# Places modulo 256 bytes for split weights and sums in a two-layer hybrid block, and other orders for the second MLP's w2

## The chip, the cores and the metric

The kernel runs on one core of a Trainium2 chip. The time is the device time of one execution in microseconds, the median of several runs. A profile of one execution gives start and length of each engine's instructions. TensorE (PE) multiplies; VectorE (DVE) and ScalarE (ACT) prepare operands and take results out of PSUM; GpSimd (POOL) does little here; SyncE (SP) issues the loads of the weights.

## What is computed

Two layers on x of 256 tokens by 2048 features, float32 throughout:

```python
def reference(x, ...):
    h = x
    for layer in range(2):
        if layer == 0:
            h = h + stick_breaking_attention(rms_norm(h, sb_norm_g[0]), sb_w_qkv[0], sb_w_out[0])
        else:
            h = h + native_sparse_attention(rms_norm(h, nsa_norm_g[0]), nsa_w_in[0], ..., nsa_w_out[0])
        h = h + sqrelu_mlp(rms_norm(h, mlp_norm_g[layer]), mlp_w1[layer], mlp_w2[layer])
    return h

def sqrelu_mlp(h, w1, w2):          # w1: 2048 x 8192, w2: 8192 x 2048
    return jnp.square(jax.nn.relu(h @ w1)) @ w2
```

The first attention has 16 heads of width 128; the second has 16 query heads in 4 groups with a compressed, a selected and a windowed branch and gates.

## The kernel before, in words

**Split operands.** TensorE multiplies float32 in a rounded form. The kernel writes each operand as a sum, hi + lo: hi is the rounded copy, lo the difference, rounded too. A product of two operands is then three products, hi by hi, lo by hi and hi by lo. For a weight this is done on the way: SP loads a piece of 512 KB into a `raw` tile (L132, five buffers), ScalarE copies it to `hi` (L125, four buffers), VectorE subtracts to `lo` (L127, four buffers), TensorE uses both. Activations lie split in `xs` (xhi and xlo side by side) and in `yhi` and `ylo`.

**Kinds of product.** Each product has a stationary operand of 128 by 128, loaded by a weight load (PEld), and a moving operand of 128 rows with up to 512 columns.
- Wide products with x (`proj_T2`, L193 and L199; `proj_T2h`, L213 and L219): the weight is stationary, xs moves. hi takes xhi and xlo at once, 512 columns; lo takes xhi alone, 256 columns.
- Ordinary chunks (`chunk_N`, L147): the weight moves, 512 columns, and x or y is stationary. A chunk is two rows of 128 of the weight by 512 columns, 12 products.
- Strassen chunks (`chunk_S`, L243 to L268): one of the four column blocks of w2 is multiplied by Strassen's scheme for two-by-two blocks, 7 products for 8, in 256 columns, so 21 with the split. VectorE makes four combinations of the weight's blocks in `ts` (L243, L247, L248), which are split like a weight into hi and lo (L125, L127). Three blocks go in without a combination: `shi` is their rounded copy (ScalarE, L246), `slo` their difference (VectorE, L249). `shi` and `slo` have one buffer each. The stationary operands are blocks of yhi and ylo and, for three of the seven pairs with a combination and one without, sums of y in the tile `ss`. So 12 of the 21 products have `ss`.

**The MLP.** Each layer's MLP runs over four quarters of the 8192 inner features. In a quarter, group1 makes the inner activations (four blocks of 512, each eight chunks of `proj_T2`), and squares, splits and sums them. group2 multiplies by w2: column blocks 0, 1 and 3 by ordinary chunks, block 2 by eight Strassen chunks spread among these. That is eight groups of eight Strassen chunks in the two layers.

**What sets the order.** TensorE's order is as written in the program. The tile framework's scheduler sets the orders of ScalarE, VectorE and SP from the dependencies between tiles: an instruction that writes a tile whose buffer is still read is placed, and waits, behind the last reader. Each engine then runs its instructions in that order. A tile is one unit for this: its last reader is the last reader of any part of it.

**Places.** The start of `xs`, `yhi` and `ylo` in each partition lies at 128 modulo 256 bytes; raw, hi, lo, `ts`, `shi`, `slo` and `ss` lie at 192.

Of the kernel before, what the change touches and what calls it, by code (L numbers as in the profile page):

```python
# [8 lines left out]
F32 = mybir.dt.float32  # L9
# [30 lines left out]
def hybrid_kernel(  # L40
# [8 lines left out]
    small = ctx.enter_context(tc.tile_pool(name="small", bufs=2))  # L49
    wraw = ctx.enter_context(tc.tile_pool(name="wraw", bufs=5))  # L50
# [15 lines left out]
    g0 = cpool.tile([KD, P], F32, name="g0")  # L66
    nc.scalar.dma_start(g0, sb_norm_g[0].rearrange("(k p) -> k p", p=P))
    grows = cpool.tile([P, P], F32, name="grows")
# [19 lines left out]
    def other_gains():  # L88
        nc.vector.memset(grows, 0.0)
        nc.sync.dma_start(grows[G_M0:G_NSA, :], mlp_norm_g.rearrange("l (k p) -> (l k) p", p=P))  # L90
        nc.sync.dma_start(grows[G_NSA:G_Q, :], grow(nsa_norm_g[0]))
        nc.sync.dma_start(grows[G_Q:G_K, :], nsa_q_norm_g)
        nc.sync.dma_start(grows[G_K:G_K + 3, :], nsa_k_norm_g[0])
        pgt = att.tile([P, NB], F32, tag="att", name="pgt2")
        nc.tensor.transpose(pgt[:, :P], grows, ident)
        nc.vector.tensor_copy(gT[:, KD:], pgt[:, KD:P])
        nc.vector.tensor_scalar(gq, gT[:, G_Q:G_K], SCALE, None, op0=OP.mult)
# [25 lines left out]
    def split(raw):  # L123
        hi = whi.tile(raw.shape, F32R, tag="hi", name="hi")
        nc.scalar.activation(hi, raw, AF.Copy)  # L125
        lo = wlo.tile(raw.shape, F32R, tag="lo", name="lo")
        nc.vector.tensor_tensor(lo, raw, hi.bitcast(F32), op=OP.subtract)  # L127
        return hi, lo

    def load(src, k0, nk, n0, nn):  # L130
        raw = wraw.tile([P, nk, nn], F32, tag="raw", name="raw")
        nc.sync.dma_start(  # L132
            raw, src[k0 * P:(k0 + nk) * P, n0:n0 + nn].rearrange("(k p) n -> p k n", p=P)
        )
        return raw

    def load_split(*where):
        return split(load(*where))
# [4 lines left out]
    def chunk_N(ps, src, k0, n0, first, last, ahi, alo, koff=0, by_token=False):  # L143

        hi, lo = src if isinstance(src, tuple) else load_split(src, k0, KC, n0, NB)
        tiles = [(kk, k0 - koff + kk, t) for kk in range(KC) for t in range(NT)]
        mm = lambda a, b, k, t, s, e: nc.tensor.matmul(ps[t], a[:, k, t * P:(t + 1) * P], b, start=s, stop=e)  # L147
        if by_token:

            half = [slice(0, NB // 2), slice(NB // 2, NB)]  # L150
            for t, c in [(0, slice(0, NB)), (1, half[0]), (1, half[1])]:
                for a, w in ((ahi, hi), (alo, hi), (ahi, lo)):
                    for kk in range(KC):
                        k = k0 - koff + kk
                        nc.tensor.matmul(
                            ps[t][:, c], a[:, k, t * P:(t + 1) * P], w[:, kk, c], start=False, stop=True,
                            skip_group_check=True,
                        )
            return
# [26 lines left out]
    def proj_T2(ps, src, n0):  # L186


        for k0 in range(0, KD, KC):
            hi, lo = load_split(src, k0, KC, n0, NB)  # L190
# [14 lines left out]
    def proj_T2h(src, n0):  # L205
# [3 lines left out]
        for k0 in range(0, KD, KH):  # L209
            hi, lo = load_split(src, k0, KH, n0, W)  # L210
# [23 lines left out]
    def chunk_S(ps, src, k0, n0, first, last, ahi, alo, shi, slo, koff=0):  # L234
# [9 lines left out]
        hi = wsum.tile([P, 3 * W], F32R, tag="shi", name="shi", bufs=1)  # L244
        lo = wsum.tile([P, 3 * W], F32R, tag="slo", name="slo", bufs=1)
# [40 lines left out]
    def add_S(nb, bs, ps, pool):  # L286

        W = NB // 2
        u = pool.tile([P, 2, W], F32, tag="u", name="u", bufs=1)
        v = pool.tile([P, 2, W], F32, tag="v", name="v", bufs=1)  # L290
# [127 lines left out]
    def mlp(l, layer, junk, done, last=None):  # L418
# [37 lines left out]
        def group2(fg, plain, strassen, end):  # L456
# [8 lines left out]
            for nb, i in order:  # L465
# [12 lines left out]
                if i == 0:  # L478
                    ps = [bank(*plain) for _ in range(NT)]
                out = last is not None and end and nb == 3  # L480
                chunk_N(ps, w2, k0, nb * NB, i == 0, i == NK - (2 if out else 1), yhi, ylo, koff=fg * KD,
                        by_token=out and i == NK - 1)
# [207 lines left out]
    pes = cpool.tile([2 * CL, P], F32, name="pes")  # L690
# [403 lines left out]
```

## Time and profile before

| | |
|---|---|
| time, median of 3 runs | 2201.65 us (2200.3 to 2204.76) |
| time of the profiled execution | 2201.79 us |
| its span | 2200.1 us |
| TensorE busy in the span | 2187.0 us (99%), 11922 products |
| VectorE, ScalarE busy | 1537.9 us (70%), 1204.4 us (55%) |
| first attention, 0 to 397 us: TensorE busy | 392.8 us |
| first MLP, 397 to 1100 us | 703.0 of 703.0 us |
| second attention, 1100 to 1490 us | 388.6 of 390.0 us |
| second MLP, 1490 to 2200 us | 702.6 of 710.0 us |

The profile's instructions are followed by their line in the kernel. The name of a tile stands without its buffer number: `att<-hi,ss` is a product into a PSUM bank of the pool att with moving operand hi and stationary operand ss. A product's recorded length holds its way through the array; products overlap, so their pace is read from one start to the next.

### The profile page before, as it was taken

How to read it: one execution, taken by the hardware profiler on the slowest of the kernel's cores; microseconds unless marked ns; L12 is line 12 of the kernel's file. 1: busy time of each engine (PE TensorE's matmuls, PEld its weight loads, DVE VectorE, ACT ScalarE, POOL GpSimd, SP SyncE). 2: the span in 40 equal slices, each digit the busy share in tenths (PEclk: the TensorE clock that was granted, in tenths of full speed). 3: DMA queues.
4: the chain of work that ended last, by engine and by line, in shares of the span. 5: the costliest groups of instructions: out<-in, count | busy, mean ns of one | idle time of the engine just before them, and what ended most of it. 6: DMA issues, size and time to landing. Idle time of an engine off the chain costs nothing.

```text
span 2200.1 us, 31289 instructions
## 1 busy us (share of the span) xinstructions
PE 2187.0 (99%) x11922; PEld 1875.4 (85%) x11922; DVE 1537.9 (70%) x2096; ACT 1204.4 (55%) x1697; POOL 42.6 (2%) x75
## 2 busy tenths in 40 slices
PE   9999999999999999999999999999999999999998
PEld 9888888888888888888887888888888888888887
DVE  5656655677667677668777777756776776777775
ACT  5565665555455455455555666655554554554553
POOL 0000000000000000000000011000000000000000
PEclk9999999999999999999999999999999999999999
DMA  7655555665665665665667554456556656656654
GB/s 233 207 165 172 165 171 182 182 192 184 205 190 175 215 190 178 215 191 174 213 184 219 153 144 139 134 169 183 181 183 214 188 184 207 189 174 220 189 174 155
DMA packets 260767, 405.98 MB, mean 185 GB/s; under 512 B 13188, under 2 KB 91912, under 8 KB 260616
## 3 DMA queue, kind: packets, MB, share of 16 engines
q1 hardware_dynamic: 259800, 403.52, 60.2%
q8 instruction: 93, 1.52, 0.3%
q10 hardware_dynamic: 816, 0.46, 0.1%
q14 instruction: 58, 0.48, 0.1%
HBM read 401.83 MB, written 2.10 MB: 184 GB/s over the span
## 4 chain that ended last, share of the span: by engine, by line
PE 98%; DVE 1%; DMA 0%; POOL 0%; ACT 0%; issue 0%; DVEq 0%; ACTq 0%; POOLq 0%
PE acc L147 31%; PE att L147 13%; PE acc L193 11%; PE att L193 11%; PE acc L213 5%; PE acc L199 5%; PE att L199 5%; PE att L268 4%; PE acc L268 3%; PE acc L219 3%; PE acc L176 2%; PE att L926 1%; PE att L331 1%; PE att L918 0%; DMA raw<-in_mlp_w_dram 0%; PE att L919 0%
## 5 line engine op out<-in xcount | busy, mean ns | idle before, releaser
L127 DVE TENSOR_TENSOR lo<-raw,hi 128x1024 fp32r<-128x1024 f32 x687 | 836.6, 1222 | 380.3 <-ACT hi L125 358.1
L125 ACT ACTIVATE hi<-raw 128x1024 fp32r<-128x1024 f32 x687 | 724.8, 1057 | 656.3 <-PE acc L147 208.5
L193 PE MATMUL acc<-xs,hi 128*128 128x512 f32 x1024 | 259.8, 396 | 0.0
L193 PE MATMUL att<-xs,hi 128*128 128x512 f32 x1024 | 259.1, 395 | 0.0
L147 PE MATMUL acc<-hi,yhi 128*128 128x512 f32 x640 | 251.7, 394 | 0.0
L147 PE MATMUL acc<-hi,ylo 128*128 128x512 f32 x640 | 250.6, 392 | 0.0
L193 PEld LDWEIGHTS acc<-xs,hi 128*128 128x128 f32 x1024 | 183.0, 188 | 34.7 <-DVE h L387 0.3
L193 PEld LDWEIGHTS att<-xs,hi 128*128 128x128 f32 x1024 | 183.2, 188 | 34.5
L147 PE MATMUL acc<-hi,xs 128*128 128x512 f32 x704 | 178.6, 394 | 0.0
L147 PE MATMUL acc<-lo,yhi 128*128 128x512 f32 x640 | 174.1, 393 | 0.0
L147 PEld LDWEIGHTS acc<-hi,xs 128*128 128x128 f32 x704 | 130.5, 188 | 27.6
L147 PE MATMUL att<-hi,ylo 128*128 128x512 f32 x380 | 149.7, 394 | 0.0
L147 PE MATMUL att<-hi,yhi 128*128 128x512 f32 x380 | 149.4, 393 | 0.0
L199 PEld LDWEIGHTS acc<-xs,lo 128*128 128x128 f32 x1024 | 135.9, 188 | 11.6
L199 PEld LDWEIGHTS att<-xs,lo 128*128 128x128 f32 x1024 | 135.9, 188 | 11.6
L147 PEld LDWEIGHTS acc<-lo,yhi 128*128 128x128 f32 x640 | 119.6, 188 | 25.8 <-issue 0.4
L147 PEld LDWEIGHTS acc<-hi,ylo 128*128 128x128 f32 x640 | 120.3, 188 | 24.5 <-DVE ylo L318 0.2
L147 PEld LDWEIGHTS acc<-hi,yhi 128*128 128x128 f32 x640 | 120.2, 188 | 24.3 <-ACT yhi L317 0.2
L199 PE MATMUL acc<-xs,lo 128*128 128x256 f32 x1024 | 137.6, 277 | 0.0
L199 PE MATMUL att<-xs,lo 128*128 128x256 f32 x1024 | 137.5, 277 | 0.0
L243 DVE TENSOR_TENSOR ts<-raw 128x512 f32<-128x512 f32 x64 | 44.3, 692 | 128.9 <-DMA raw<-in_mlp_w_dram 128.9
L125 ACT ACTIVATE hi<-ts 128x1024 fp32r<-128x1024 f32 x64 | 67.9, 1061 | 114.4 <-DVE ts L248 86.3
(305 smaller groups left out, 3064.9 us busy)
## 6 DMA issues: line engine op xcount, KB each, us to landing
raw<-in_mlp_w_dram SPq DMA_DIRECT2D x512, 512.0 KB, 4.2
raw<-in_sb_w_qkv_dram SPq DMA_DIRECT2D x95, 512.0 KB, 4.2
raw<-in_nsa_w_in_dram SPq DMA_DIRECT2D x50, 512.0 KB, 3.6
raw<-in_sb_w_out_dram SPq DMA_DIRECT2D x32, 512.0 KB, 3.9
raw<-in_nsa_w_in_dram SPq DMA_DIRECT2D x64, 256.0 KB, 3.4
raw<-in_nsa_w_out_dram SPq DMA_DIRECT2D x32, 512.0 KB, 3.9
w1t<-in_nsa_cmp_w_dram SPq DMA_DIRECT2D x8, 512.0 KB, 4.8
h<-in_x_dram SPq DMA_DIRECT2D x8, 256.0 KB, 4.5
```

Of the source, the lines that this page charges most:

```text
L125: nc.scalar.activation(hi, raw, AF.Copy)
L127: nc.vector.tensor_tensor(lo, raw, hi.bitcast(F32), op=OP.subtract)
L147: mm = lambda a, b, k, t, s, e: nc.tensor.matmul(ps[t], a[:, k, t * P:(t + 1) * P], b, start=s, stop=e)
L176: nc.tensor.matmul(o, w[:, kk, m * P:(m + 1) * P], x[:, k0 + kk, :], start=s, stop=e, skip_group_check=True)
L193: nc.tensor.matmul(ps[m], hi[:, kk, m * P:(m + 1) * P], xs[:, k0 + kk, :, :].rearrange("p a t -> p (a t)"), start=k0 + kk == 0, stop=k0 + ...
L199: nc.tensor.matmul(ps[m][:, :T], lo[:, kk, m * P:(m + 1) * P], xhi[:, k0 + kk, :], start=False, stop=k0 + kk == KD - 1, skip_group_check=True,
L213: nc.tensor.matmul(ps[m], hi[:, kk, m * P:(m + 1) * P], xs[:, k0 + kk, :, :].rearrange("p a t -> p (a t)"), start=k0 + kk == 0, stop=k0 + ...
L219: nc.tensor.matmul(ps[m][:, :T], lo[:, kk, m * P:(m + 1) * P], xhi[:, k0 + kk, :], start=False, stop=k0 + kk == KD - 1, skip_group_check=True,
L243: nc.vector.tensor_tensor(ts[:, :2, :], flat[:, W:3 * W].rearrange("p (a n) -> p a n", a=2), b12, op=OP.subtract)
L268: nc.tensor.matmul(ps[i], a, w, start=s, stop=e, skip_group_check=True)
L331: nc.tensor.transpose(ps[:, j * T + t * P:j * T + (t + 1) * P], h[:, t, (kp + j) * P:(kp + j + 1) * P], ident)
L926: nc.tensor.transpose(ptp[:w, j * P:(j + 1) * P], src(j), ident)
```

## The change

The tiles `hi` and `lo` get 64 elements of padding, and `split` takes an offset in elements for each: with 16 (FAR) the data starts at 192 modulo 256 bytes, as before, with 36 (NEAR) at 16. The wide products L193 and L213 use NEAR for hi and FAR for lo. The tile sizes move other tiles: `ss` now starts at 128, raw and `ts` at 128, and some small tiles of the second attention shift by 64; xs, yhi and ylo stay at 128. `shi` and `slo` become the halves of one tile `both` with one buffer, each half starting at 192. The two tiles u and v of `add_S` become one that shares its place with `pre`; the small tiles of gains and position rows share a place.

In the second layer's MLP, w2's ordinary chunks take their hi and lo at other places. In the first quarter column blocks 0, 1 and 3 have 128, 240 and 160; in the other three quarters 192, 128 and 240. In these three quarters the order of a chunk's twelve products changes too. Before, for each weight row and token half, hi·yhi and hi·ylo alternate, then the four lo·yhi follow. In the second quarter (way 1) all four hi·yhi, all four hi·ylo, then the four lo·yhi; in the third (way 2) the same sorted by token half; in the fourth (way 3) the three products of each pair follow each other. The last column block of the last quarter keeps its order.

```diff
@@ -47,6 +47,7 @@
     nc = tc.nc
     cpool = ctx.enter_context(tc.tile_pool(name="cpool", bufs=1))
     small = ctx.enter_context(tc.tile_pool(name="small", bufs=2))
+    small.tile([P, 48], F32, name="gap", bufs=1)
     wraw = ctx.enter_context(tc.tile_pool(name="wraw", bufs=5))
     whi = ctx.enter_context(tc.tile_pool(name="whi", bufs=4))
     wlo = ctx.enter_context(tc.tile_pool(name="wlo", bufs=4))
@@ -120,10 +121,17 @@
                 pass
 
-    def split(raw):
-        hi = whi.tile(raw.shape, F32R, tag="hi", name="hi")
+
+
+    PAD = 64
+    NEAR, FAR = 36, 16
+
+    def split(raw, o=(FAR, FAR)):
+        n = KC * NB
+        view = lambda t, a: t[:, a:a + n].rearrange("p (k n) -> p k n", k=raw.shape[1])
+        hi = view(whi.tile([P, n + PAD], F32R, tag="hi", name="hi"), o[0])
         nc.scalar.activation(hi, raw, AF.Copy)
-        lo = wlo.tile(raw.shape, F32R, tag="lo", name="lo")
+        lo = view(wlo.tile([P, n + PAD], F32R, tag="lo", name="lo"), o[1])
         nc.vector.tensor_tensor(lo, raw, hi.bitcast(F32), op=OP.subtract)
         return hi, lo
 
@@ -134,15 +142,15 @@
         )
         return raw
 
-    def load_split(*where):
-        return split(load(*where))
+    def load_split(*where, o=(FAR, FAR)):
+        return split(load(*where), o)
 
     def bank(pool, tag):
         return pool.tile([P, NB], F32, tag=tag, name=tag)
 
-    def chunk_N(ps, src, k0, n0, first, last, ahi, alo, koff=0, by_token=False):
-
-        hi, lo = src if isinstance(src, tuple) else load_split(src, k0, KC, n0, NB)
+    def chunk_N(ps, src, k0, n0, first, last, ahi, alo, koff=0, by_token=False, o=(FAR, FAR), way=0):
+
+        hi, lo = src if isinstance(src, tuple) else load_split(src, k0, KC, n0, NB, o=o)
         tiles = [(kk, k0 - koff + kk, t) for kk in range(KC) for t in range(NT)]
         mm = lambda a, b, k, t, s, e: nc.tensor.matmul(ps[t], a[:, k, t * P:(t + 1) * P], b, start=s, stop=e)
         if by_token:
@@ -157,6 +165,20 @@
                             skip_group_check=True,
                         )
             return
+        if way:
+            one = lambda a, w: [(a, w, kk, k, t) for kk, k, t in tiles]
+            order = one(ahi, hi) + one(alo, hi) + one(ahi, lo)
+            if way == 2:
+                order.sort(key=lambda x: x[4])
+            if way == 3:
+                order = [x for j in range(len(tiles)) for x in order[j::len(tiles)]]
+            seen = set()
+            for j, (a, w, kk, k, t) in enumerate(order):
+                mm(a, w[:, kk, :], k, t, first and t not in seen, last and all(x[4] != t for x in order[j + 1:]))
+                seen.add(t)
+            pump()
+            pump()
+            return
         for part in [tiles]:
             for kk, k, t in part:
                 mm(ahi, hi[:, kk, :], k, t, first and kk == 0, False)
@@ -187,7 +209,7 @@
 
         for k0 in range(0, KD, KC):
-            hi, lo = load_split(src, k0, KC, n0, NB)
+            hi, lo = load_split(src, k0, KC, n0, NB, o=(NEAR, FAR))
             tiles = [(kk, m) for kk in range(KC) for m in range(NB // P)]
             for kk, m in tiles:
                 nc.tensor.matmul(
@@ -207,7 +229,7 @@
         ps = [bank(acc, "acc") for _ in range(2)]
         KH, W = 2 * KC, NB // 2
         for k0 in range(0, KD, KH):
-            hi, lo = load_split(src, k0, KH, n0, W)
+            hi, lo = load_split(src, k0, KH, n0, W, o=(NEAR, FAR))
             tiles = [(kk, m) for kk in range(KH) for m in range(2)]
             for kk, m in tiles:
                 nc.tensor.matmul(
@@ -241,8 +263,8 @@
         ts = wsum.tile([P, 4, W], F32, tag="ts", name="ts")
         b12 = flat[:, 3 * W:].unsqueeze(1).to_broadcast([P, 2, W])
         nc.vector.tensor_tensor(ts[:, :2, :], flat[:, W:3 * W].rearrange("p (a n) -> p a n", a=2), b12, op=OP.subtract)
-        hi = wsum.tile([P, 3 * W], F32R, tag="shi", name="shi", bufs=1)
-        lo = wsum.tile([P, 3 * W], F32R, tag="slo", name="slo", bufs=1)
+        both = wsum.tile([P, 6 * W + PAD], F32R, tag="both", name="both", bufs=1)
+        hi, lo = [both[:, FAR + i * 3 * W:FAR + (i + 1) * 3 * W] for i in range(2)]
         nc.scalar.activation(hi, flat[:, :3 * W], AF.Copy)
         nc.vector.tensor_tensor(ts[:, 2, :], ts[:, 0, :], flat[:, 2 * W:3 * W], op=OP.add)
         nc.vector.tensor_tensor(ts[:, 3, :], flat[:, :W], ts[:, 2, :], op=OP.subtract)
@@ -286,8 +308,8 @@
     def add_S(nb, bs, ps, pool):
 
         W = NB // 2
-        u = pool.tile([P, 2, W], F32, tag="u", name="u", bufs=1)
-        v = pool.tile([P, 2, W], F32, tag="v", name="v", bufs=1)
+        uv = pool.tile([P, 4, W], F32, tag="pre", name="uv", bufs=1)
+        u, v = uv[:, :2, :], uv[:, 2:, :]
         hb = [h[:, t, nb * NB:(nb + 1) * NB] for t in range(NT)]
         nc.scalar.activation(u[:, 0, :], ps[0], AF.Copy)
         nc.vector.tensor_tensor(v[:, 0, :], ps[5], u[:, 0, :], op=OP.add)
@@ -478,8 +500,11 @@
                 if i == 0:
                     ps = [bank(*plain) for _ in range(NT)]
                 out = last is not None and end and nb == 3
+                a = 16
+                if l == 1:
+                    a = ((0, 28, 8), (16, 0, 28))[fg > 0][(0, 1, 1, 2)[nb]]
                 chunk_N(ps, w2, k0, nb * NB, i == 0, i == NK - (2 if out else 1), yhi, ylo, koff=fg * KD,
-                        by_token=out and i == NK - 1)
+                        by_token=out and i == NK - 1, o=(a, a), way=fg if l == 1 and not out else 0)
                 if i == NK - 1:
                     if out:
                         add_out(nb, ps, last)
```

The change moves instructions on VectorE and ScalarE around the Strassen chunks. This is VectorE in the first layer's third quarter, before. raw_7900 is the weight piece of the Strassen chunk that TensorE starts at 876.47 us, raw_7971 that of the next one, which it starts at 884.43 us; the `lo` from raw are of ordinary chunks between them:

```order
L243 TENSOR_TENSOR ts_7973<-raw_7971 128x512
L247 TENSOR_TENSOR ts_7973<-ts_7973,raw_7971 128x256
L249 TENSOR_TENSOR slo_7905<-raw_7900,shi_7904 128x768
L127 TENSOR_TENSOR lo_7939<-raw_7935,hi_7937 128x1024
L248 TENSOR_TENSOR ts_7973<-raw_7971,ts_7973 128x256
L127 TENSOR_TENSOR lo_7957<-raw_7953,hi_7955 128x1024
L127 TENSOR_TENSOR lo_7983<-ts_7973,hi_7981 128x1024
L243 TENSOR_TENSOR ts_8066<-raw_8064 128x512
L249 TENSOR_TENSOR slo_7976<-raw_7971,shi_7975 128x768
L127 TENSOR_TENSOR lo_8010<-raw_8006,hi_8008 128x1024
```

The same stretch of VectorE now; raw_7880 and raw_7950 are the two pieces, and L271 with the output `both` is the low half:

```order
L265 TENSOR_TENSOR ts_7952<-raw_7950 128x512
L269 TENSOR_TENSOR ts_7952<-ts_7952,raw_7950 128x256
L270 TENSOR_TENSOR ts_7952<-raw_7950,ts_7952 128x256
L135 TENSOR_TENSOR lo_7918<-raw_7914,hi_7916 128x1024
L271 TENSOR_TENSOR both_7884<-raw_7880,both_7884 128x768
L135 TENSOR_TENSOR lo_7936<-raw_7932,hi_7934 128x1024
L135 TENSOR_TENSOR lo_7961<-ts_7952,hi_7959 128x1024
L265 TENSOR_TENSOR ts_8044<-raw_8042 128x512
L135 TENSOR_TENSOR lo_7988<-raw_7984,hi_7986 128x1024
L271 TENSOR_TENSOR both_7954<-raw_7950,both_7954 128x768
```

The low half of each Strassen chunk stands one `lo` of an ordinary chunk further back, the first of the two also behind the last `ts` step. ScalarE in the same stretch, before:

```order
L125 ACTIVATE hi_7910<-ts_7902 128x1024
L246 ACTIVATE shi_7904<-raw_7900 128x768
L125 ACTIVATE hi_7937<-raw_7935 128x1024
L125 ACTIVATE hi_7955<-raw_7953 128x1024
L125 ACTIVATE hi_7981<-ts_7973 128x1024
L246 ACTIVATE shi_7975<-raw_7971 128x768
L125 ACTIVATE hi_8008<-raw_8006 128x1024
```

And now, where L268 is the high half in `both`:

```order
L133 ACTIVATE hi_7889<-ts_7882 128x1024
L133 ACTIVATE hi_7916<-raw_7914 128x1024
L268 ACTIVATE both_7884<-raw_7880 128x768
L133 ACTIVATE hi_7934<-raw_7932 128x1024
L133 ACTIVATE hi_7959<-ts_7952 128x1024
L133 ACTIVATE hi_7986<-raw_7984 128x1024
L268 ACTIVATE both_7954<-raw_7950 128x768
```

The high half too stands one copy of an ordinary chunk further back. The order of the loads on SP is the same.

More of the change, by code (lines that the diff above doesn't have):

```diff
@@ L65, in hybrid_kernel @@
     G_SB, G_M0, G_M1, G_NSA, G_Q, G_K = 0, KD, 2 * KD, 3 * KD, 64, 65
-    g0 = cpool.tile([KD, P], F32, name="g0")
+    g0 = small.tile([P, P], F32, tag="grow", name="g0", bufs=1)[:KD, :]
     nc.scalar.dma_start(g0, sb_norm_g[0].rearrange("(k p) -> k p", p=P))
-    grows = cpool.tile([P, P], F32, name="grows")
     grow = lambda g: g.rearrange("(k p) -> k p", p=P)
@@ L88, in other_gains @@
     def other_gains():
+        grows = small.tile([P, P], F32, tag="grow", name="grows", bufs=1)
         nc.vector.memset(grows, 0.0)
@@ L688, in hybrid_kernel @@
         out_proj(sb_w_out[0], "m0", G_M0)
-    pes = cpool.tile([2 * CL, P], F32, name="pes")
+    pes = small.tile([P, P], F32, tag="grow", name="pes", bufs=1)[:2 * CL, :]
     nc.scalar.dma_start(pes, nsa_cmp_pe[0].rearrange("a l d -> (a l) d"))
```

## The prediction

> **What bounds the kernel now.** I read the page first (busy shares, chain by engine), then the waits of TensorE, then the chain piece by piece for the pace of each kind of product, and last the timeline of one Strassen chunk on VectorE, TensorE and the DMA queue.
>
> ```profile
> PE 2187.0 (99%) x11922; PEld 1875.4 (85%) x11922; DVE 1537.9 (70%) x2096; ACT 1204.4 (55%) x1697; POOL 42.6 (2%) x75
> PE 98%; DVE 1%; DMA 0%; POOL 0%; ACT 0%; issue 0%; DVEq 0%; ACTq 0%; POOLq 0%
> PE acc L268 <- DVE slo L249: 3.4, 3, 2.6
> ```
>
> TensorE is busy for 99% of the span and is 98% of the chain that ended last. Its largest wait is 3.4 us in three places, all for the low half of a Strassen chunk. So two things can move the time: the pace of the products themselves, and new waits of TensorE for what VectorE and ScalarE prepare. The page's row of TensorE clocks is 9 in all slices, so no clock change lies in it.
>
> The change touches both. Pace first, from the chain of waits (start us, us, what):
>
> ```profile
> 584.29 1.86 PE att L193 x8
> 586.15 0.91 PE att L199 x8
> 131.47 10.08 PE acc L147 x44
> 871.14 5.49 PE acc L147 x24
> 876.63 2.46 PE att L268 x21
> ```
>
> A wide product with x (L193, 512 columns) takes 1.86/8 = 232.5 ns from start to start. A product of the ordinary w2 and projection chunks (L147, also 512 columns, also 128 by 128) takes 10.08/44 = 229.1 or 5.49/24 = 228.8 ns. Same size, same clock, 3.6 ns apart. What differs is where the operands lie (the places here are the start addresses that the two programs give their tiles): in L193 the moving operand (xs) lies at 128 modulo 256 bytes in each partition and the stationary one (hi) at 192; in L147 it is the other way round.
>
> **The change part by part.**
>
> *The wide products.* Their hi goes from 192 to 16, against xs at 128. No product of the kernel before has that pair of places, so the cost is bounded by the nearest rows.
>
> ```profile
> L193 PE MATMUL att<-xs,hi 128*128 128x512 f32 x1024 | 259.1, 395 | 0.0
> L213 PE MATMUL acc<-xs,hi 128*128 128x512 f32 x512 | 130.2, 396 | 0.0
> L193 PE MATMUL att<-xs,hi x1024: 388/396/398, 420.9 to 2081.7; 128*128 128x512 f32 x171
> ```
>
> There are 2 x 1024 of L193 (the other half writes acc) and 512 of L213: 2560 products. The third row gives shortest, median and longest. If each went as the shortest does, the gain is 8 ns each, 2560 x 8 = 20.5 us; if each went as the longest, a loss of 2 ns each, 5 us. I take the pace of L147, 3.6 ns less, because it is the same product size with its operands at another relation of places: 2560 x 3.6 = 9.2 us saved. A new hi place alters no instruction of ScalarE or VectorE, and these stages show no wait of TensorE for hi or lo, so the gain counts in full.
>
> *The sums of y.* ss goes from 192 to 128. In a Strassen chunk it is the stationary operand against moving operands at 192, that is, at the same place now, and 64 bytes apart after.
>
> ```profile
> L268 PEld LDWEIGHTS att<-hi,ss x192: 192/192/192, 501.7 to 2006.7; 128*128 128x128 f32 x192
> L268 PE MATMUL att<-hi,ss x192: 283/283/283, 501.9 to 2006.8; 128*128 128x256 f32 x192
> L268 PE MATMUL att<-shi,yhi x64: 276/276/276, 501.2 to 2005.8; 128*128 128x256 f32 x64
> L268 PE MATMUL att<-hi,yhi 128*128 128x256 f32 x32 | 8.8, 276 | 0.0
> ```
>
> Same line, the same moving tile hi, the same 256 columns: 283 ns against ss (at 192), 276 ns against yhi (at 128). Twelve of a chunk's 21 products have ss, over 64 chunks 768. At 7 ns each that is 5.4 us saved. This is the best supported term: after the change these products stand exactly as those with yhi do. Its bounds are 0 (should something other than the place make ss slow) and 5.4.
>
> Against both terms stands a rule of the Trainium skill, "SBUF — State Buffer", section "SBUF: two separate sides": TensorE's ports never wait on another user, and the table of the section after it gives the loading of weights a second, independent read port; by that rule the place of an operand is worth nothing and both terms are 0. The trace does not agree: 283 against 276 ns, with nothing but the stationary tile different. No page states a rule on places modulo 256 bytes.
>
> *The second layer's w2.* In its four groups hi and lo go to 128, 240 or 160 in the first group, and to 192, 128 or 240 in the other three, in which (but for the last block) the order of a chunk's twelve products changes too: by kind, by token, or per tile hi·hi, lo·hi, hi·lo. This is 1152 products of L147; 384 of them come to lie with both operands at 128. The nearest row with both operands at one place (192 both) and 512 columns is this:
>
> ```profile
> L642 PE MATMUL att<-sh,tri x8: 389/395/398, 99.0 to 330.5; 128*128 128x512 f32 x8
> L147 PE MATMUL acc<-hi,yhi 128*128 128x512 f32 x640 | 251.7, 394 | 0.0
> ```
>
> 395 against 394 ns: 1 ns on 384 products is 0.4 us. By the spread of the first row (389 to 398) the bounds on 1152 products are -5.8 to +4.6 us. I take +0.5. The third order asks for lo at the third product of a chunk and not at the ninth, six products or 1.4 us sooner. TensorE shows no wait for L127's lo today, so this is put at nothing; if that cover is gone it costs up to 1.4 us in each of the last group's 16 chunks of that order, and it is late there only where VectorE is late for the Strassen chunks too.
>
> *One tile for both halves.* This is not in the words of the change. shi and slo, two tiles of one buffer each, become the halves of `both`, one tile of one buffer. ScalarE's write of the next chunk's high half must now wait for the last product with the previous low half (the 17th of 21), not for the last one with the high half (the 6th). The scheduler answers by placing the high and low halves later on both engines: on VectorE a low part of an ordinary chunk (L127) now stands ahead of the Strassen low half. The chunk that TensorE starts at 884.43 us, on VectorE, on the DMA queue and on TensorE:
>
> ```profile
> 873.48 0.69 DVE L243 TENSOR_TENSOR ts<-raw 128x512 f32<-128x512 f32 x1 [2.61 <-DMA raw<-in_mlp_w_dram]
> 874.55 0.95 DVE L249 TENSOR_TENSOR slo<-raw,shi 128x768 fp32r<-128x768 f32 x1
> 875.42 1.22 DVE L127 TENSOR_TENSOR lo<-raw,hi 128x1024 fp32r<-128x1024 f32 x1
> 876.55 0.42 DVE L248 TENSOR_TENSOR ts<-raw,ts 128x256 f32<-128x256 f32 x1
> 883.96 0.69 DVE L243 TENSOR_TENSOR ts<-raw 128x512 f32<-128x512 f32 x1 [4.55 <-DMA raw<-in_mlp_w_dram]
> 884.57 0.95 DVE L249 TENSOR_TENSOR slo<-raw,shi 128x768 fp32r<-128x768 f32 x1
> 885.44 1.22 DVE L127 TENSOR_TENSOR lo<-raw,hi 128x1024 fp32r<-128x1024 f32 x1
> ```
>
> ```profile
> 875.53 0.37 SPq L132 DMA_DIRECT2D raw<-in_mlp_w_dram  x1
> 876.66 0.37 SPq L132 DMA_DIRECT2D raw<-in_mlp_w_dram  x1
> 878.13 0.37 SPq L132 DMA_DIRECT2D raw<-in_mlp_w_dram  x1
> ```
>
> ```profile
> 884.43 0.28 PE L268 MATMUL att<-shi,yhi 128*128 128x256 f32 x1
> 886.07 0.39 PE L268 MATMUL att<-slo,yhi 128*128 128x256 f32 x2
> 886.29 0.28 PE L268 MATMUL att<-slo,ss 128*128 128x256 f32 x1
> ```
>
> The low half is done at 884.57 + 0.95 = 885.52 and TensorE needs it at 886.07: a margin of 0.55 us. Behind this stands a loop. The low half of one chunk ends at 875.50 and frees a raw buffer; 0.03 us later SP issues the next load; the load's data starts ts at 883.96 after 4.55 us in which VectorE only waits; and ts stands ahead of the next low half, in the order written for VectorE. What the change adds is one L127 ahead of the low half, 876.55 - 875.42 = 1.13 us to the next start (and in some chunks the last ts, 876.89 less 876.55, about 0.3). The low half is then done at 886.65 where 886.07 is needed, if the load lands as before; the load itself is issued later too, since the raw buffer is freed later in the turn before.
>
> How many chunks have so little margin? Eight chunks make a group, there are eight groups, and in the timeline the fifth and seventh of a group are the tight ones. Four more of them, low half and need:
>
> ```profile
> 709.55 0.95 DVE L249 TENSOR_TENSOR slo<-raw,shi 128x768 fp32r<-128x768 f32 x1
> 902.99 0.95 DVE L249 TENSOR_TENSOR slo<-raw,shi 128x768 fp32r<-128x768 f32 x1
> 1804.47 0.95 DVE L249 TENSOR_TENSOR slo<-raw,shi 128x768 fp32r<-128x768 f32 x1
> 1823.76 0.95 DVE L249 TENSOR_TENSOR slo<-raw,shi 128x768 fp32r<-128x768 f32 x1
> ```
>
> ```profile
> 711.71 0.39 PE L268 MATMUL acc<-slo,yhi 128*128 128x256 f32 x2
> 904.72 0.39 PE L268 MATMUL att<-slo,yhi 128*128 128x256 f32 x2
> 1805.55 0.43 PE L268 MATMUL acc<-slo,yhi 128*128 128x256 f32 x2
> 1824.76 0.51 PE L268 MATMUL acc<-slo,yhi 128*128 128x256 f32 x2 [0.33 <-DVE slo L249]
> ```
>
> Margins: 1.21, 0.78, 0.13 and 0.05 us, with the 0.55 above five. Delayed by one step of 1.13 us, the five lack 0, 0.35, 1.00, 1.08 and 0.58, a mean of 0.60; sixteen tight chunks (two in eight groups) make 9.6 us. Delayed by two steps and a ts (2.6 us: its own, and that of the turn before through the load) they lack 1.39, 1.82, 2.47, 2.55 and 2.05, a mean of 2.06, or 33 us. I take the middle, 21 us: the first load of the turn is issued later, but the third at 878.13 follows work that keeps its place in sum, and a chunk that waited hands part of its delay back to the seventh. The high half's later write (free after 886.29 + 0.28 = 886.57) has the next chunk's 8 us before it and costs nothing by itself.
>
> The rest (u and v in one tile, small tiles sharing a place) has no place in the chain and is put at 0.
>
> **The sum.** The profiled execution took 2201.79 us (its span 2200.1), the median shown is 2201.65, so one stands for the other. -9.2 - 5.4 + 0.5 + 21 = +6.9: 2208.7, forecast **2209 us**, slower by 0.3%.
>
> **The rivals.**
>
> *Placement wins.* The wide products fall to their shortest row (-20.5) and the waits cost a single step (9.6): -20.5 - 5.4 + 0.5 + 9.6 = -15.8, 2186 us. With the wide products at my pace it is -4.5, 2197. For it: 21 us of waits lean on a loop with slack in its loads; against it: margins of 0.05 to 0.55 us leave no room. It needs waits under about 10 us.
>
> *A draw.* Waits of 10 to 19 us against 14 saved: 2197 to 2206.
>
> *Place decides nothing.* ss is slow for its values or its loads (192 ns), L193 for its own run of eight; then only the waits are left: 2201.8 + 21.5 = 2223. For it: L642, at one place, is no slower than L147. Against it: 276 and 283 on one line. The rule of the Trainium skill's "SBUF — State Buffer" named above is this case.
>
> *The new place is worse.* Wide products at their longest (+5): 5 - 5.4 + 21.5 = +21, 2223. It decides from 16 against 128 being slower than 192 against 128.
>
> **How the numbers follow.** A measurement of this kernel tells about 0.2% (4.4 us) from no change. Forecast (waits outweigh the places, 2206 to 2217) 0.42; place decides nothing 0.13; new place worse 0.05; draw 0.20; placement wins 0.20. So slower 0.60, same 0.20, faster 0.20. The range reaches from 2190, which keeps most of the winning case, to 2226, which holds the two worst ones.
>
> **What would show it.** In the profile after: TensorE's waits for the low half of `both` rise from 3.4 to near 21 us, mostly in the fifth and seventh chunks; eight wide products take 1.83 us in the chain and not 1.86; products with ss fall to 276 ns and the chunk's 21 from 2.46 to 2.38 us. If the waits stay under 10 us the sign is wrong; if eight wide products stay at 1.86, the place is not what sets their pace.

## The result

The changed kernel takes 2231.76 us (median of 4 runs, 2227.62 to 2234.1) against 2202.24 us for the kernel before: slower by a ratio of 1.0131, 95% interval 1.0113 to 1.0150, or 29.5 us. I had forecast slower, but by 7 us, and the time lies above my range. The profiled execution took 2227.62 us, the fastest of the four; its span is 25.8 us longer than that of before.

From the page of the changed kernel, busy times and the chain that ended last by engine:

```profile
PE 2198.4 (99%) x11922; PEld 1881.6 (85%) x11922; DVE 1537.0 (69%) x2096; ACT 1202.9 (54%) x1697; POOL 42.6 (2%) x75
PE 89%; DMA 5%; DVE 4%; issue 1%; ACT 0%; POOL 0%; DVEq 0%; ACTq 0%; SPq 0%; POOLq 0%
```

TensorE has the same 11922 products and is busy for 11.4 us more; the chain, 98% TensorE before, now runs for 9% through loads and VectorE. Two things happened, then: TensorE waits for prepared operands, and its products became slower and not faster. The waits of TensorE in the changed kernel (total us, times, longest):

```profile
PE att L290 <- DVE both L271: 9.7, 10, 1.5
PE acc L290 <- DVE both L271: 7.4, 5, 2.2
PE acc L290 <- ACT both L268: 0.6, 1, 0.6
```

17.7 us in place of 3.4. The longest, on VectorE, on TensorE, and in the view by stretches (the third number from the right is TensorE's granted clock, ahead of the DMA share and the GB/s):

```profile
717.04 0.69 DVE L265 TENSOR_TENSOR ts<-raw 128x512 f32<-128x512 f32 x1 [5.42 <-DMA raw<-in_mlp_w_dram]
717.65 1.22 DVE L135 TENSOR_TENSOR lo<-raw,hi 128x1024 fp32r<-128x1024 f32 x1
718.79 0.95 DVE L271 TENSOR_TENSOR both<-raw,both 128x768 fp32r<-128x768 f32 x1
```

```profile
715.83 0.28 PE L290 MATMUL acc<-both,yhi 128*128 128x256 f32 x1
717.36 0.28 PE L290 MATMUL acc<-hi,ylo 128*128 128x256 f32 x1
719.79 0.55 PE L290 MATMUL acc<-both,yhi 128*128 128x256 f32 x2 [2.15 <-DVE both L271]
720.36 0.84 PE L290 MATMUL acc<-lo,ss 128*128 128x256 f32 x3
```

```profile
716.00:719.00 3.00, 1.64 (x14) 1.43 (x13) 1.96 (x3) 0.17 (x1) 0.00 (x0) 1.00 0.01 5
719.00:723.00 4.00, 3.21 (x12) 2.82 (x13) 3.93 (x6) 1.34 (x2) 0.00 (x0) 0.64 0.73 218
723.00:727.00 4.00, 4.00 (x18) 3.28 (x17) 1.91 (x3) 1.51 (x2) 0.00 (x0) 0.93 0.88 264
```

This is the loop that the prediction described: VectorE waits 5.42 us for a load, then does ts, then the `lo` that the change put ahead, then the low half. But the listed idle time is not all that a wait costs. It is counted from the recorded end of the product before, 0.28 us after that product's start, where in a run the next one starts after 0.11 to 0.12 us. And two products with the low half take 0.39 us in a run (711.71 in the prediction) but 0.50 to 0.51 us behind a wait (1824.76 there, 702.26 in e9 below), so the second of them is some 0.11 us late too. In all a wait costs some 0.28 us beside its listed length.

Behind this wait TensorE also has a granted clock of 0.64 over 4 us; the three lo by ss products take (721.00 - 720.36)/3 = 213 ns each, where 113 to 118 ns is usual. A clock at 0.64 for 4 us loses 1.4 us, the 4 us behind it another 0.3. The Trainium skill's "TensorE: Matmul & The Clock Gate", section "What's actually happening", says that the clock is halved after an idle window of about 3.4 us and comes back after about 3.4 us of sustained work. The second half agrees with the trace, where the slow products last from 720.14 to about 723.5 us; the first does not, since the idle time was only 2.15 us. For the difference between the two kernels this stretch counts nothing, though: the profiled execution of the kernel before has one too, behind its longest wait of 2.6 us, with a clock of 0.79 over 8 us, which is the same 1.7 us.

```profile
2150.00:2158.00 8.00, 7.80 (x31) 6.42 (x32) 4.37 (x7) 2.85 (x3) 0.00 (x0) 0.79 0.62 199
```

The wide products in the chain of waits of the changed kernel (start us, us, what), L215 the 512-column ones and L221 the 256-column ones behind them:

```profile
586.08 1.86 PE att L215 x8
587.94 0.94 PE att L221 x8
588.89 1.87 PE att L215 x8
590.76 0.92 PE att L221 x8
```

The wide ones did not get faster (1.86 before), and the 256-column ones, of which the change moved nothing, got slower (0.91 before). The same for the Strassen chunks, shortest, median and longest:

```profile
L290 PE MATMUL att<-hi,ss x192: 276/279/280, 503.6 to 2034.7; 128*128 128x256 f32 x192
L290 PE MATMUL att<-both,yhi x128: 275/279/392, 502.9 to 2035.2; 128*128 128x256 f32 x128
```

The products with ss fell from 283 to 279 ns, but those with yhi, at unmoved places, rose from 276 to 279. Averaging the start-to-start times in the two traces (times with a wait, a restart or the slow clock in them left out) gives the balance, each a mean difference times a number of products: wide products 232.7 to 233.4 ns, +1.8 us; the 256-column ones behind them 114.0 to 116.5 and 114.4 to 116.3, +6.2; Strassen products 117.2 to 116.5, -1.0; ordinary products with y 228.8 to 229.4, +1.8, and those with x 230.4 to 229.7, -0.8. That is 8.0 us. With 14.3 us more of waits, and 0.28 us for each of 13 more waits (16 against 3), 3.6 us, it comes to 25.9 of the 25.8 us.

### The profile page after: what moved, and what is told of

It reads as the page before. It is cut to its first block, busy times and chain, and to the rows that moved or that the text cites. A ratio compares the mean times of both kernels' runs of the same rounds, so it can differ in the third digit from the quotient of the medians.

```text
span 2225.9 us, 31234 instructions
## 1 busy us (share of the span) xinstructions
PE 2198.4 (99%) x11922; PEld 1881.6 (85%) x11922; DVE 1537.0 (69%) x2096; ACT 1202.9 (54%) x1697; POOL 42.6 (2%) x75
## 4 chain that ended last, share of the span: by engine, by line
PE 89%; DMA 5%; DVE 4%; issue 1%; ACT 0%; POOL 0%; DVEq 0%; ACTq 0%; SPq 0%; POOLq 0%
PE acc L155 27%; PE acc L215 11%; PE att L215 10%; PE att L155 10%; PE acc L235 5%; PE acc L221 5%; PE att L221 5%; DMA raw<-in_mlp_w_dram 5%; PE acc L241 3%; PE acc L290 2%; PE att L290 2%; DVE lo L135 2%; PE acc L198 2%; DVE both L271 1%; PE att L951 1%
## 5 line engine op out<-in xcount | busy, mean ns | idle before, releaser
L215 PE MATMUL acc<-xs,hi 128*128 128x512 f32 x1024 | 260.5, 396 | 0.0
L215 PE MATMUL att<-xs,hi 128*128 128x512 f32 x1024 | 259.7, 396 | 0.0
L155 PE MATMUL acc<-hi,yhi 128*128 128x512 f32 x640 | 244.1, 394 | 0.0
L155 PE MATMUL acc<-hi,ylo 128*128 128x512 f32 x640 | 242.8, 392 | 0.0
L215 PEld LDWEIGHTS att<-xs,hi 128*128 128x128 f32 x1024 | 183.7, 188 | 35.7
L215 PEld LDWEIGHTS acc<-xs,hi 128*128 128x128 f32 x1024 | 183.5, 188 | 35.8 <-DVE h L409 0.3
L221 PEld LDWEIGHTS att<-xs,lo 128*128 128x128 f32 x1024 | 137.9, 188 | 11.2
L221 PEld LDWEIGHTS acc<-xs,lo 128*128 128x128 f32 x1024 | 137.8, 188 | 11.2
L155 PEld LDWEIGHTS acc<-lo,yhi 128*128 128x128 f32 x640 | 119.5, 188 | 26.2 <-issue 0.4
L221 PE MATMUL att<-xs,lo 128*128 128x256 f32 x1024 | 140.1, 279 | 0.0
L221 PE MATMUL acc<-xs,lo 128*128 128x256 f32 x1024 | 140.0, 279 | 0.0
L155 PE MATMUL att<-hi,yhi 128*128 128x512 f32 x380 | 137.9, 394 | 0.0
L155 PE MATMUL att<-hi,ylo 128*128 128x512 f32 x380 | 137.7, 393 | 0.0
```

What stands on the lines that cost most here:

```text
L215: nc.tensor.matmul(ps[m], hi[:, kk, m * P:(m + 1) * P], xs[:, k0 + kk, :, :].rearrange("p a t -> p (a t)"), start=k0 + kk == 0, stop=k0 + ...
L221: nc.tensor.matmul(ps[m][:, :T], lo[:, kk, m * P:(m + 1) * P], xhi[:, k0 + kk, :], start=False, stop=k0 + kk == KD - 1, skip_group_check=True,
```

## The experiments

The kernel before was run beside each group of kernels on the same chip. Ratios are to it, with 95% intervals. In the experiments' kernels the halves of `both` are again called shi and slo where they are two tiles.

### e1: two tiles again

```diff
-        both = wsum.tile([P, 6 * W + PAD], F32R, tag="both", name="both", bufs=1)
-        hi, lo = [both[:, FAR + i * 3 * W:FAR + (i + 1) * 3 * W] for i in range(2)]
+        hi = wsum.tile([P, FAR + 3 * W], F32R, tag="shi", name="shi", bufs=1)[:, FAR:]
+        lo = wsum.tile([P, 3 * W + PAD - FAR], F32R, tag="slo", name="slo", bufs=1)[:, :3 * W]
```

> The changed kernel with the two halves of `both` as two tiles again, at the same places (192 modulo 256). Theory (the one tile makes the waits): TensorE's waits for the halves fall from 17.7 us to the 3 or 4 us of the kernel before, and the time falls by about 16 to 18 us to about 2214 us. Rival (the waits come from the places or the w2 orders, not from the tile): the time stays near 2231 us.

2206.91 us, ratio 1.0026 (1.0014 to 1.0039). The one tile costs 1.0131 - 1.0026, over 1% or 23 us, more than expected. The waits:

```profile
PE acc L290 <- DVE slo L271: 1.8, 2, 1.1
PE att L290 <- DVE slo L271: 0.2, 1, 0.2
```

So 15.7 us of waits went and 23 to 25 us of time. In the two profiled executions, whose spans differ by 20.8 us, most of that adds up: 15.7 us of waits, 3.6 us for 13 waits fewer, and 1.1 us for Strassen products at 115.7 and not 116.5 ns make 20.4. (Each of the two has one stretch of slow clock, e1 with 0.66 from 15 to 20 us.) That the medians differ by more may be the clock: the mean granted clock of a whole run is 0.998 in three of the changed kernel's four runs and 0.999 in all six of e1, and 0.001 is an estimated 2.2 us. And a small slowdown, 0.26%, stays, which is the places' and orders' doing.

### e2: the kernel before, with one tile

```diff
-        hi = wsum.tile([P, 3 * W], F32R, tag="shi", name="shi", bufs=1)
-        lo = wsum.tile([P, 3 * W], F32R, tag="slo", name="slo", bufs=1)
+        both = wsum.tile([P, 6 * W], F32R, tag="both", name="both", bufs=1)
+        hi, lo = [both[:, i * 3 * W:(i + 1) * 3 * W] for i in range(2)]
```

> The kernel before with shi and slo in one tile, all places as before. Theory (the one tile makes the waits): waits of TensorE for the halves of 14 to 25 us in place of 3.4, time about 2202 + 18 = 2220 us. Rival (the waits belong to the places): no more than 2204 us.

2224.09 us, ratio 1.0116 (1.0100 to 1.0132), with these waits:

```profile
PE acc L268 <- DVE both L249: 9.7, 8, 2.0
PE att L268 <- DVE both L249: 8.4, 7, 1.7
PE acc L268 <- ACT both L246: 1.2, 2, 0.9
```

The places are those of the kernel before, and chunks without a wait keep its pace (117.4 ns per product). The tile alone brings the waits for the halves from 3.4 to 19.3 us and the time up by 23 to 26 us. Taken away from the change or added to the kernel before, the price is the same. That settles the cause of most of the slowdown.

### e3: the wide products' hi back at 192

```diff
-            hi, lo = load_split(src, k0, KC, n0, NB, o=(NEAR, FAR))
+            hi, lo = load_split(src, k0, KC, n0, NB)
```

and the same in `proj_T2h`.

> The changed kernel with the wide products' hi back at 192 modulo 256. Theory (hi at 16 slows the wide products and the 256-column products behind them, which after the change take 0.93 us per eight and not 0.91): about 6 us less, 2225 us, eight 256-column products back at 0.91 us. Rival (the pace comes from something else, such as the padded buffers): 2231 us and 0.93 us.

2226.21 us, ratio 1.0127 (1.0108 to 1.0145). Against the change's 1.0131 the time doesn't tell; the mean granted clock was lower in these runs too, 0.996 to 0.998 against 0.998 to 0.999. The pace does tell. The chain of waits of e3:

```profile
587.15 1.86 PE att L215 x8
589.01 0.91 PE att L221 x8
```

```profile
PE att L290 <- DVE both L271: 10.3, 9, 1.6
PE acc L290 <- DVE both L271: 9.5, 7, 2.2
```

Eight 256-column products are back at 0.91 us. The mean times of wide and 256-column products are back at 232.7 and 114.0 ns; the waits are 2.1 us longer than in the changed kernel. The price of hi at 16 comes out more cleanly from e1 and e10, which differ by it alone and hardly wait: 1.0026 - 0.9991 is 0.35%, 7.7 us, and the means above make 8.0.

### e5 and e10: the sums of y alone, then w2 added

e5 is e1 with the wide hi at FAR as in e3 and without the w2 places and orders:

```diff
-                if l == 1:
-                    a = ((0, 28, 8), (16, 0, 28))[fg > 0][(0, 1, 1, 2)[nb]]
...
-                        by_token=out and i == NK - 1, o=(a, a), way=fg if l == 1 and not out else 0)
+                        by_token=out and i == NK - 1, o=(a, a), way=0)
```

> The changed kernel with two tiles for the halves, the wide products' hi at 192 and w2 as in the kernel before: what is left is the move of ss from 192 to 128 (and the padding). Theory (a Strassen chunk has two paces, 113.3 or 117.8 ns per product, handed on from the products before it, and the ss products at 192 went at 120): the chunks start at 113.3 ns and fall to 117.8 after a wait of TensorE; 2.38 or 2.47 us per chunk against 2.46, in all 0 to 5 us less than before, 2196 to 2201 us. Rival (the page of before read plainly: 283 against 276 ns on 768 products): 2195.5 us in any case, all chunks at 2.38 us.

2196.15 us, ratio 0.9980 (0.9970 to 0.9989): 4.4 us faster than before, interval 2.4 to 6.6. This part of the change is a gain, and the prediction's 5.4 us lies in it. In the chain the chunks do go at 2.38 us until TensorE waits for one, and at 2.47 behind it (e5, first group; the piece of 1.10 us is the end of the chunk that waited):

```profile
537.76 0.96 DVE slo L271
538.72 0.04 issue
538.76 1.10 PE att L290 x7
539.86 8.24 PE acc L155 x36
548.10 2.47 PE att L290 x21
550.58 5.49 PE acc L155 x24
556.07 2.48 PE att L290 x21
```

A chunk thus has two paces with every operand at the same place: 113.3 ns per product (2.38 us) or 117.8 (2.47).

e10 keeps the w2 lines and is otherwise e5.

> As e5, with the second layer's w2 in the orders and places of the change. Theory (places 128 and 240 hand the Strassen chunks the slow pace, 117.8 for 113.3 ns on 21 products in some 28 chunks, 2.6 us, and 160 and 240 are 2 to 4 ns slower themselves): about 4 to 5 us more than e5, 2200 to 2201 us. Rival (as predicted, by the length of the products alone): 0.5 us more, 2196.7 us.

2199.2 us, ratio 0.9991 (0.9982 to 1.0001): 0.11% or some 2.5 us above e5, between the two expectations, and the intervals overlap, so the time alone does not show it. The trace shows both suspected sources. In the second layer the chunks behind ordinary products at 128 or 240 go at the slow pace with no wait before them. Its chain of waits in the second quarter of that layer:

```profile
1791.95 5.48 PE att L155 x24
1797.43 2.48 PE acc L290 x21
1799.90 5.48 PE att L155 x24
1805.38 2.48 PE acc L290 x21
```

Twenty-four ordinary products at 128 take 5.48 us, as at 192 (5.49), and the Strassen chunk between them 2.48 and not 2.38. In the first quarter of the layer, which keeps the old order of products, the chunks behind 128 and 240 are slow as well and those behind 160 are not: the place does this, and not the order. Over all, Strassen products go from 113.9 to 115.1 ns (1.6 us) and ordinary products with y from 229.1 to 229.4 (0.9 us), together the 2.5 us. (e10 also has 1.2 us less of waits than e5, and one stretch of slow clock, from 16.5 us, that e5 has not.)

### e4 and e8: all sixteen places

Both have two tiles for the halves, and w2 in its old order. In e4, `proj_T2` gets the place of hi as an argument, another for each block of four columns, and the ordinary w2 chunks another for each column block:

```diff
+                i = (16 * l + 4 * fg + fb) * (5 if l else 1) + 3 * l
+                proj_T2(ps, w1, fg * D + fb * NB, 4 * (i % 16))
...
+                a = 4 * (7 * (12 * l + 3 * fg + (0, 1, 1, 2)[nb]) % 16)
```

> The halves as two tiles; each block of four columns of the wide products in the MLPs has hi at another place, all 16 multiples of 16 bytes modulo 256, each in two blocks; each column block of the ordinary w2 chunks has hi and lo at one of the 16 places, w2's orders as before. If the place relative to the other operand sets the pace, the start-to-start time of a product is a function of the place, from about 226 to 236 ns, repeated in both blocks of a place. If pace is a matter of how a run of products is entered, blocks with one place differ as much as blocks with different places.

One execution, 2208.71 us. Mean start-to-start times from its trace, in ns (xs, yhi and ylo are at 128; for the first two columns both blocks of a place):

| place of hi | wide, hi there | the 256-column ones behind, lo at 192 | ordinary w2, hi and lo there |
|---|---|---|---|
| 0 | 232.3, 232.1 | 115.2, 115.4 | 232.4 |
| 16 | 233.4, 233.4 | 116.7, 116.6 | 233.2 |
| 48 | 230.5, 230.6 | 114.4, 114.4 | 233.4 |
| 64 | 229.4, 229.6 | 114.0, 114.1 | 233.1, 233.1 |
| 112 | 229.5, 229.7 | 115.9, 116.0 | 236.2 |
| 128 | 229.6, 229.8 | 117.3, 117.7 | 227.3, 228.1 |
| 160 | 233.5, 233.3 | 116.5, 116.2 | 233.2 |
| 192 | 232.8, 232.8 | 114.6, 114.1 | 228.9 |
| 224 | 234.8, 234.8 | 114.2, 114.2 | 233.4 |
| 240 | 233.1, 233.1 | 117.7, 117.7 | 231.1, 230.9 |

The place does set the pace of long runs: two blocks of one place, far apart in time, agree within 0.5 ns for the wide products, while places differ by up to 5 ns. (The ordinary ones agree within 1 ns but at one place: at 176, not in the table, 233.0 and 230.0.) But it is no function of the distance. Among the wide products 64 and 192 are both 64 bytes from xs and differ by 3.3 ns, and 128, where xs itself lies, is one of the fast places. The place of hi also moves the pace of the products behind, which do not use hi. In the chain of waits of e4, hi at 64 and hi at 16:

```profile
936.57 1.83 PE att L215 x8
938.41 0.91 PE att L221 x8
```

```profile
780.64 1.86 PE att L215 x8
782.50 0.94 PE att L221 x8
```

e8 has the wide hi at 64 throughout and moves the lo of the wide products and the parts of the Strassen chunks through the places.

> Wide hi at 64, the lo of the wide products at each of 16 places in two blocks; each Strassen chunk has its high, low, and both split parts of ts at one of 16 places, each in four chunks. If the place alone sets the pace, chunks with one place have one pace. If the pace is handed on, chunks at one place show two paces, by what went before.

One execution, 2201.42 us. For lo, 64 and 192 are the best (a wide and a 256-column run of eight each take 2.756 to 2.762 us); the others take 2.766 to 2.821. Strassen chunks at most places show one pace in all their chunks, such as 113.8 ns at 64 (but for one with two steps of some 220 ns in it) and 119.5 at 224; at 0, 80, 208 and 192 they show two, at 192, the place that the kernels use, 113.3 in one chunk and 117.9 in three. Both expectations hold, then, each at some places.

### e9: one wait made on purpose

e5, with one chunk's low half computed seven times, the same result each time:

```diff
+        for _ in range(again):
+            nc.vector.tensor_tensor(lo, flat[:, :3 * W], hi.bitcast(F32), op=OP.subtract)
```

`again` is 7 in the third chunk of the first layer's second group, else 1.

> As e5, with the low half of one Strassen chunk (the third of the second group of the first layer) computed seven times over on VectorE, the same result each time: one wait of TensorE of some us in a group that had none. Theory (the pace of a Strassen chunk is handed on, and a wait of TensorE changes it): the two chunks before stay at 113.3 ns per product, the five behind it go at 117.8, and the next group is back at 113.3. Rival (pace is a matter of places alone): all the others stay at 113.3 ns.

One execution, 2198.0 us. The wait came. It is shown in the view of waits from 680 to 770 us, on TensorE, and in the view by stretches; then the chain behind it:

```profile
PE acc L291 <- DVE slo L272: 2.2, 1, 2.2
702.26 0.50 PE L291 MATMUL acc<-slo,yhi 128*128 128x256 f32 x2 [2.23 <-DVE slo L272]
702.50:706.00 3.50, 3.50 (x21) 3.04 (x21) 3.47 (x5) 0.59 (x1) 0.00 (x0) 1.00 0.65 202
```

```profile
701.26 0.96 DVE slo L272
702.22 0.04 issue
702.26 0.62 PE acc L291 x3
702.88 2.52 PE att L155 x11
705.40 2.38 PE acc L291 x21
707.78 5.49 PE att L155 x24
713.27 2.38 PE acc L291 x21
```

The chunks behind stay at 2.38 us, and the granted clock stays at 1.00 (the third number from the right above). My theory in its strict form, that a wait puts the chunks behind it to the slow pace, falls. What the traces of the eight other kernels with ss at 128 bear out is weaker. Taking pairs of chunks of one group that both follow ordinary products at 192: where the first had no wait, the second kept its pace in 311 of 314 pairs; where the first had a wait, the second was slow in 33 of 38. So the pace is handed on, and a wait draws it anew, mostly, not always, to the slow one. What decides the draw is open.

### e6, e7 and e11: a faster version

e6 is e5 with `NEAR, FAR = 48, 16`, the wide hi at 64.

> As e5, with the wide products' hi at 64 modulo 256. By the sweep of places (2.748 us for sixteen products with hi at 64 and lo at 192, 2.777 with hi at 192) 320 chunks gain 0.029 us each: 9.3 us less than e5. If the sweep's blocks do not carry over to the whole kernel: as e5.

2193.17 us, ratio 0.9958 (0.9943 to 0.9973): about 0.2% below e5, less than expected. The wide products go at 229.6 ns as in the sweep, which with the 256-column ones behind them is 5.8 us less than in e5; in `proj_T2h`, which the sweep had not covered, the gain is 0.6 us. TensorE's waits for the low halves are 5.3 us in all, longest in the last groups, where e5 has 3.7.

e7 is e6 with `o=(0, 0)`, place 128, for the chunks in `proj_N` and `out_proj`.

> As e6, with the ordinary chunks of the attention's projections (1152 products with x less a quarter, 768 with y) at 128, where their stationary operand lies. By the sweep 227.5 ns in place of 229 to 231: 2 to 4 us less than e6. If 227.5 holds only between the w2's Strassen chunks: as e6.

2190.4 us, ratio 0.9948 (0.9931 to 0.9965); the step of 2 to 3 us from e6 is as expected, though the intervals overlap.

e11 is e7 with the Strassen chunks of the last groups further apart:

```diff
-                if si < NK and i >= (3 + 1.75 * si if end else 4 + 2.25 * si):
+                if si < NK and i >= (3 + 2 * si if end else 4 + 2.25 * si):
```

> As e7, with the Strassen chunks of each layer's last group one per 2 ordinary chunks and not per 1.75. Theory (the last groups' waits of TensorE, 4.9 us in three places, come from the closer spacing): these waits fall below 2 us, and with them the slow pace behind; 3 to 6 us less than e7, 2185 to 2187 us. Rival (the later end of the last Strassen chunk holds up what follows the layer): no gain.

2183.47 us, ratio 0.9923 (0.9906 to 0.9939): by the ratios 17 us faster than the kernel before and 46 us faster than the change. Against e7 it is 5.5 us, within the 3 to 6 us expected, though the intervals just overlap; the trace is clearer. TensorE is busy for 2171.6 us, and the chain of waits in the last group is this:

```profile
2103.31 2.38 PE acc L290 x21
2105.69 5.49 PE att L155 x24
2111.18 2.38 PE acc L290 x21
```

TensorE waits for no Strassen chunk any more, and all 64 run at 2.38 us.

## Why the prediction was wrong, point by point

In steps of the ratios the runs give each term its own size: ss at 128 -4.4 us (e5; forecast -5.4), w2 +2.4 (e10 less e5; forecast +0.5), hi at 16 +7.7 (e1 less e10; forecast -9.2), the one tile +23 (the change less e1; forecast +21). Together that is +29, where the forecast was +6.9.

**The one tile: right in kind, and nearly in size.** The prediction named `both`, the `lo` ahead of the low half, and the loop through the load, and put 21 us on it. e1 and e2 give 23 us or a little more. Inside that sum two errors cancelled, which is luck. The waits are 17.7 us, 14 more than before, and not 21 more; and the step "-9.2 - 5.4 + 0.5 + 21" had no term for what a wait costs beside its length: the 0.28 us at each restart, the slower chunks behind it, and perhaps, by the runs' mean clocks, some slow clock. The prediction read "no clock change" from the page's row of clocks, whose slices of 55 us hide the stretch at 2150 us. And in the profile the waits are in the third to fifth chunks of a group and none in a seventh: the fifth was right. Nor was the margin of the last line it read (1823.76) 0.05 us: the product at 1824.76 had already waited 0.33 us for that low half.

The delay was also larger than the upper bound of "two steps and a ts (2.6 us)". In the second group's fifth chunk the low half started 2.16 us before it was needed (709.55 against 711.71). After the change it starts 1.32 us behind the need (718.79, against 717.36 + 0.11 = 717.47, when the product before it would have let it go). That is a shift of 3.5 us: 1.14 for the `lo` that stands ahead (717.65 to 718.79), and some 2.3 for a load that comes later. The last load that SP issued before it went out 8.30 us ahead of the need (703.41) and now 6.96 ahead (710.51), 1.3 us of the 2.3; the ts started 5.5 and now 6.5 us behind that issue, which is the other 1.0, and why it took longer is not shown.

**The wide products: the failing step.** "I take the pace of L147, 3.6 ns less, because it is the same product size with its operands at another relation of places": measured, the wide products are 0.7 ns slower, +1.8 us, not -9.2. The even worse omission is that the 256-column products behind them were costed at nothing, since their places do not change. They cost +6.2 us. Together that is +8 where -9.2 stood, 17 us of the 22 to 23 us that the forecast was off. The inference from one pair of places to another was not supported: by e4's table, places at one distance differ as much as others. The bounds taken from the spread of one place's own products (-20.5 to +5) hold for the wide products alone, but not for the two kinds together. The sign that it named would have misled as well: eight wide products did stay at 1.86 us, yet the place does set their pace, 1.83 us at 64 and 1.86 at 16 in e4.

**The sums of y: right alone, lost in company.** -5.4 was forecast, e5 measured -4.4 (2.4 to 6.6). In the changed kernel it came to -1.0, since "these products stand exactly as those with yhi do" held, but those with yhi then stood worse: at these places a chunk has two paces, and the waits and w2's places put some 45 of its 64 chunks to the slow one. With ss at 192 the same waits did no lasting harm: in e2 the chunks are back at the pace of before at once or one chunk after a group's last wait.

**w2: mis-sized.** +0.5 was forecast, from the products' own lengths; e10 less e5 gives about 2.5 us. Missing was what the ordinary products hand on to the Strassen chunks between them, 1.6 us of it.

**The rivals.** "The new place is worse" (2223 us, chance 0.05) was nearest: the wide stretches did get worse, by 8 us and not 5, and through the lo products, which that rival did not have. "Place decides nothing", which the prediction drew from the rule of the Trainium skill's "SBUF — State Buffer", section "SBUF: two separate sides", is refuted by e4: places alone move the wide products by 5 ns.

## What to carry to other kernels

Two tiles made into one also join their dependencies: the writer of the first half then waits for the last reader of the second, and a scheduler moves it; give each half its own tile, even where they shall lie side by side. Where TensorE is the bound, waits cost more than their listed length (here 16 us listed came to 21 to 22 us in the profiled executions and 23 to 26 in the medians), so count the restarts and the pace behind them too. Before a slow clock is blamed for a difference, look whether the other kernel has the same stretch. The place of an operand modulo 256 bytes can be worth 2 to 4% of a product's time between the best and the worst, but not by a rule of distance that one pair of rows gives: sweep the places in one run, block by block, and take the products that follow into the sum.

## What the runs showed of the hardware that was not expected

The pace of float32 products of one shape depends reproducibly on the places of their operands modulo 256 bytes: 229.4 to 234.8 ns for 512 columns with the weight stationary, 227.3 to 236.2 with the weight moving. It is in part a state: 256-column products with every operand at the same places run at 113.3 or 117.8 ns each for a whole chunk, and keep the one or the other over the products between. A wait takes some 0.28 us more of TensorE than its listed idle time. The granted clock fell to 0.64 over 4 us behind one idle time of 2.15 us, and stayed at 1.00 behind another of 2.23 us (e9).
